# Six staggered weight tiles, a padded activation pitch, split first loads and dummy products in a two-layer encoder on one core

## The chip, the core and the metric

The kernel runs on one core of a Trainium2 chip. That core has five engines that run side by side and tell each other by semaphores when a tile is ready: TensorE (PE in the profile; its weight loads stand on a row of their own, PEld), VectorE (DVE), ScalarE (ACT), GpSimd (POOL) and SyncE (SP), which here only issues the transfers from the chip's memory. TensorE multiplies a stationary operand, which a weight load has put into its array, with a moving operand, and adds into an accumulation bank (PSUM). All other tiles lie in the on-chip memory SBUF, 128 partitions wide; an address in this text is a byte offset within a partition.

The metric is device time in microseconds (us), the median over three runs: 1684.95 us before (1684.54 to 1685.41).

## The reference

The input is 256 positions of 2048 channels, in float32. Two layers follow each other; the part of the reference that sets the work is the sequence of projections:

```python
h = rms_norm(x, norm_w[0])
a_q, a_i, a_ff, a_fb, a_g, b_u, b_g = split_cols(h @ w_in, EV_SIZES)   # 7 x 2048 columns
a_out = hgrn2_mixer(a_q, a_i, a_ff, a_fb, lb, hgrn_nw) * silu(a_g)     # chunked gated recurrence
b_out = fourier_mixer(b_u, fw, fb) * silu(b_g)                         # Re(DFT2), then a map per group
x = x + concatenate([a_out, b_out]) @ w_out                            # 4096 -> 2048
h = rms_norm(x, norm_w[1])
c_in, c_b, c_c, c_g, d_z, d_xbc, d_dt = split_cols(h @ w_in, OD_SIZES)
c_out = c_b * conv3(c_c * c_in) * silu(c_g)
d_out = ssd_mixer(d_xbc, d_dt, d_z, ...)                               # Mamba-2 scan, both directions
x = x + concatenate([c_out, d_out]) @ w_out
return rms_norm(x, final_norm_w)
```

Every weight is used once for all 256 positions, so 314 MB of weights pass through the core, and the four large projections are nearly all of the arithmetic.

## The kernel before

**Products in two parts.** TensorE multiplies in a single-pass form of float32 with fewer bits (`float32r`). To keep the accuracy, a weight tile is split into `hi`, its rounded value, and `lo`, the rest; an activation is split in the same way into `s = 0` and `s = 1`. A product is hi times both parts and lo times the first. The activations of a layer lie in `xx` (16 channel tiles, each with 2 parts of 256 positions, 2048 bytes per tile), the inputs of an output projection in `mm` (32 such tiles).

**The weight ring.** The weights come in halves of 128 x 1024 numbers (512 KB), 562 in all, in the order of the list `halves`. `load()` issues the transfer of one half into one of 5 raw tiles. `fetch()` makes hi on ScalarE (L132) and lo on VectorE (L133), into one of 3 pairs, the ring: hi0, lo0, hi1, lo1, hi2, lo2. `half()` hands out the next pair and runs `fetch()` up to 4 halves ahead. A pair is written again only when TensorE has read it, and a raw tile when lo is made. The last eight halves use three further pairs from the pool `fin`.

**The three streams of products.** `gemm_half` (L164, L167) uses the weights as stationary operand: 8 products with hi and 512 moving columns (both parts of `xx`), then 8 with lo and 256 columns. 402 halves go this way. `tproduct` (L183), the output projections, has `mm` stationary and the weights moving, 12 products of 512 columns per half, 128 halves. The value projection (L508) has `xx` stationary, 12 products per half, 32 halves; its first eight halves are the kernel's first work.

**What sets the order.** The code is written as one sequence; each engine takes its own instructions from it in an order that the build lays down, and waits in that order. `later(n, fn)` puts small work (scores, transposes, convolutions, norms) n halves behind the place where it is written. Transfers are all issued by SyncE, in order, on a set of eight completion semaphores, so that a transfer also waits until the one eight issues ahead of it has landed.

**The start.** L258 to L271: the parameters, then four raw halves and eight x tiles of two channel tiles each. For every x tile, `split_by` makes the scaled activation `xx` on ScalarE (L223) and its remainder on VectorE (L224). In between `norm0` squares the x tiles on ScalarE (L276), and small tables of the lower bounds (L310 to L319) are made on VectorE, with an exponential on ScalarE (L314).

**Addresses.** In the built program every raw, hi and lo tile (4096 bytes each), `xx`, `mm`, `conT`, the t1 tiles (1024 bytes) and the larger working tiles start at a multiple of 512 bytes. The tile `fill` (L69) is not used by any instruction; it moves the pools behind it to such a multiple. `acT` holds, among others, the sine table `sl`, whose two parts start 8 and 4 bytes past a multiple of 512.

Of the kernel before, what the change touches and what calls it, by code (L numbers as in the profile page):

```python
# [8 lines left out]
F32 = mybir.dt.float32  # L9
F32R = mybir.dt.float32r  # L10
U32 = mybir.dt.uint32
AF = mybir.ActivationFunctionType
ALU = mybir.AluOpType
ADD, SUB, MUL, MIN, MAX = ALU.add, ALU.subtract, ALU.mult, ALU.min, ALU.max

P = 128
D = 2048
L = 256
KT = D // P
# [37 lines left out]
def encoder_kernel(ctx: ExitStack, tc, xT, xN, w_ev, w_evo, w_od, w_odo, fw, fnr, par, con, acon, tric, outN):  # L57
    nc = tc.nc
    V, S, PE = nc.vector, nc.scalar, nc.tensor

    cpool = ctx.enter_context(tc.tile_pool(name="cpool", bufs=1))
    wpool = ctx.enter_context(tc.tile_pool(name="wpool", bufs=1))
    tp = ctx.enter_context(tc.tile_pool(name="tp", bufs=1))
# [6 lines left out]

    parT = cpool.tile([P, NPAR], F32, tag="par", name="parT")
    conT = cpool.tile([P, NCON], F32, tag="con", name="conT")
    xx = cpool.tile([P, KT, 2, L], F32R, tag="xx", name="xx")
    mm = cpool.tile([P, 2 * KT, 2, L], F32R, tag="mm", name="mm")
    epsT = sp.tile([P, 1], F32, tag="eps", name="epsT")
    x1d = dpool.tile([2, P, D], F32, tag="x1d", name="x1d")
# [2 lines left out]
    def pcol(name, i):  # L79
        return parT[:, PCOL[name] + i:PCOL[name] + i + 1]  # L80
# [4 lines left out]
    lpool, N2, NPM = [], 8, 4  # L85

    def t1(name, n=L):
        return tp.tile([P, n], F32, tag="t1", name=name, bufs=18)

    def t2(name, shape=(2, L)):  # L90
        return lpool[0].tile([P, *shape], F32, tag="t2", name=name, bufs=N2)

    def psum(tag, name, bufs, shape=(512,)):
        return ps.tile([P, *shape], F32, tag=tag, name=name, bufs=bufs)
# [4 lines left out]
    def paux(name, shape=(512,)):  # L99
        return psum("px", name, 8 - NPM, shape)  # L100
# [4 lines left out]
    n = 2 * (112 + 32)  # L105
# [2 lines left out]
    state = {"load": 0, "next": 0, "use": 0}  # L108
    HK = KT // 2
    NRAW, NHL, AHEAD = 5, 3, 4  # L110
    endp = []

    def load():
        n = state["load"]
        state["load"] = n + 1
        src, i, h = halves[n]
        raw = wpool.tile([P, HK * P], F32, tag=f"raw{n % NRAW}", name=f"raw{n}")
        nc.sync.dma_start(out=raw, in_=src[i][:, h * HK * P:(h + 1) * HK * P])
        loaded[n] = raw

    def fetch():
        n = state["next"]
        state["next"] = n + 1
        if n >= state["load"]:
            load()
        raw = loaded.pop(n)
        kept = n - (len(halves) - 8)
        i = n % NHL if kept < 0 else kept % (2 * NHL)
        pool = wpool if i < NHL else endp[0]
        hi = pool.tile([P, HK * P], F32R, tag=f"hi{i}", name=f"hi{n}")  # L130
        lo = pool.tile([P, HK * P], F32R, tag=f"lo{i}", name=f"lo{n}")
        S.activation(hi, raw, AF.Copy)  # L132
        V.tensor_tensor(lo, raw, hi.bitcast(F32), SUB)  # L133
        ready[n] = (hi, lo)

    def later(n, fn):
# [15 lines left out]
    def half():  # L152

        n = state["use"]
        due(n)
        while state["next"] <= min(n + AHEAD, len(halves) - 1):
            fetch()
        state["use"] = n + 1
        return ready.pop(n)
# [46 lines left out]
    def total(name, p):  # L206

        u = t1(f"{name}_u")
        S.activation(u, p[:, L:], AF.Copy)
        V.tensor_tensor(u, p[:, :L], u, ADD)  # L210
        return u
# [5 lines left out]
    def split_by(dst, src, w=None):  # L217

        if w is None:
            S.activation(dst[:, 0], src, AF.Copy)  # L220
            V.tensor_tensor(dst[:, 1], src, dst[:, 0].bitcast(F32), SUB)
        else:
            S.activation(dst[:, 0], src, AF.Copy, scale=w)  # L223
            V.scalar_tensor_tensor(dst[:, 1], src, w, dst[:, 0].bitcast(F32), MUL, SUB)  # L224
# [20 lines left out]
    def silu(name, z):  # L245
        e = t1(f"{name}_e")
        S.activation(e, z, AF.Exp, scale=-1.0)
        V.tensor_scalar(e, e, BIG, None, MIN)
        S.activation(e, e, AF.Ln, bias=1.0)
        S.activation(e, e, AF.Exp, scale=-1.0)  # L250
        V.tensor_tensor(e, e, z, MUL)
        return e
# [2 lines left out]
    lay = ExitStack()  # L255
    ap_ = lay.enter_context(tc.tile_pool(name="ap", bufs=1))
    lpool.append(ap_)
    nc.sync.dma_start(out=parT, in_=par)  # L258
    V.memset(epsT, EPS)
    xcs = []  # L260
    for c in range(8):
        if c % 2 == 0:
            load()
        xc = t2(f"x{c}")
        nc.sync.dma_start(out=xc, in_=xT[:, 2 * c:2 * c + 2, :])
        xcs.append(xc)
    for c in range(8):
        if c % 2 == 0:
            fetch()
        for k in range(2):  # L270
            split_by(xx[:, 2 * c + k], xcs[c][:, k, :], pcol("nw0", 2 * c + k))  # L271
    rs = {}

    def norm0():
        for c in range(8):
            S.activation(xcs[c], xcs[c], AF.Square)  # L276
        for n in (4, 2, 1):
            for c in range(n):
                V.tensor_tensor(xcs[c], xcs[c], xcs[c + n], ADD)
        rs["sq"] = t1("sq_x")  # L280
        V.tensor_tensor(rs["sq"], xcs[0][:, 0, :], xcs[0][:, 1, :], ADD)
# [14 lines left out]
    with lay:  # L296
# [203 lines left out]
        for hp in range(8):  # L500
            if hp % 2 == 0:
                pv = [pmain(f"pv{hp}_{b}") for b in range(2)]
                for u in range(8):
                    hi, lo = half()
                    for k in range(2):
                        for b in range(2):
                            for n, (s_, w) in enumerate(((0, hi), (0, lo), (1, hi))):
                                PE.matmul(pv[b], lhsT=xx[:, 2 * u + k, s_, b * P:(b + 1) * P],  # L508
                                          rhs=w[:, k * 4 * P:(k + 1) * 4 * P], start=(u == 0 and k == 0 and n == 0),
                                          stop=(u == 7 and k == 1 and n == 2))  # L510
# [5 lines left out]
            for i in range(2):  # L516
                h = 2 * hp + i
# [15 lines left out]
            for i in range(2):  # L533
                h = 2 * hp + i
# [6 lines left out]


    ss1 = sp.tile([P, 2, 4], F32, tag="ss1", name="ss1")
    ones = cpool.tile([P, P], F32, tag="ones", name="ones")
    nc.gpsimd.memset(ones, 1.0)
    op = ctx.enter_context(tc.tile_pool(name="op", bufs=1))

    def tok(name, bufs=4):
        return op.tile([P, 4 * P], F32, tag="tok", name=name, bufs=bufs)
# [10 lines left out]
    for g in range(4):  # L560
# [7 lines left out]
        for b in range(2):  # L568
            V.tensor_tensor(x1[b], x1[b], po[b], ADD)
            nc.sync.dma_start(out=x1d[b, :, g * 4 * P:(g + 1) * 4 * P], in_=x1[b])  # L570
            s = tok(f"x1s{g}_{b}", 4)
# [213 lines left out]


    fin = ctx.enter_context(tc.tile_pool(name="fin", bufs=1))
    xf = cpool.tile([P, KT, 2, L], F32, tag="xx", name="xf").rearrange("p a b c -> p (a b c)")
    x2, fnT = xf[:, :2 * D].rearrange("p (b n) -> p b n", b=2), xf[:, 2 * D:3 * D]
    nc.sync.dma_start(out=fnT, in_=fnr.partition_broadcast(P))  # L790
    endp.append(fin)
# [142 lines left out]
```

## Time and profile before

| | |
|---|---|
| median of three runs | 1684.95 us (1684.54 to 1685.41) |
| the profiled execution's own time | 1684.59 us |
| its span, first to last instruction | 1682.8 us |
| TensorE busy, products | 1666.2 us, 9216 recorded |
| VectorE busy | 1247.6 us |
| ScalarE busy | 950.2 us |
| read from memory | 313.77 MB, 189 GB/s over the span with what is written |

A span is what the profiler saw of the program; the execution's own time includes some 1.8 us around it. Products are recorded longer than they hold TensorE, since the next one starts while the last one drains; the pace is therefore read from the starts. A float32 product that is not of the form `float32r` appears as two records.

### The profile page before, as it was taken

Reading aid. Unit: us, or ns where it says so; the run is one execution under the profiler, and the core shown is the slowest. Engines: PE = TensorE matmul, PEld = TensorE weight load, DVE = VectorE, ACT = ScalarE, POOL = GpSimd, SP = SyncE. Lnnn points to the kernel's source line nnn. Section 1 sums busy time; section 2 is a strip of 40 time slices with the busy share of each in tenths; the row PEclk is TensorE's granted clock in tenths of the full one; section 3 lists DMA queues with packets and bytes.
Section 4 is the critical chain, followed back from the end, with each engine's and each line's share of the span. In section 5 each row is a group of like instructions: output and inputs, shape, how many; then the busy total and the mean of one; then the engine's idle time right before and its main releaser. Section 6 shows DMA issues by size and latency. Waiting matters only on the chain.

```text
span 1682.8 us, 24794 instructions
## 1 busy us (share of the span) xinstructions
PE 1666.2 (99%) x9216; PEld 1443.0 (86%) x9216; DVE 1247.6 (74%) x2187; ACT 950.2 (56%) x1593; POOL 1.8 (0%) x13
## 2 busy tenths in 40 slices
PE   8999999999999999999999999999999999999997
PEld 6888888888888888888888888888888888888886
DVE  7868677867786788754548998888898797865554
ACT  6656555655665565644445576666665565654443
POOL 0000000000000000000000000000000000000000
PEclk9999999999999999999999999999999999999999
DMA  8555555545445545476665667656656655576553
GB/s 304 173 179 174 167 171 179 171 167 186 166 158 180 191 154 178 158 223 206 213 212 191 205 218 200 195 191 203 197 185 201 196 193 179 178 238 209 195 192 123
DMA packets 97977, 319.65 MB, mean 190 GB/s; under 512 B 10880, under 2 KB 19520, under 8 KB 97728
## 3 DMA queue, kind: packets, MB, share of 16 engines
q1 hardware_dynamic: 97856, 318.07, 57.5%
q8 instruction: 72, 1.18, 0.3%
q14 instruction: 49, 0.40, 0.1%
HBM read 313.77 MB, written 4.26 MB: 189 GB/s over the span
## 4 chain that ended last, share of the span: by engine, by line
PE 99%; DMA 0%; ACT 0%; DVE 0%; ACTq 0%; issue 0%; SPq 0%
PE pz L164 10%; PE o L183 10%; PE pz L167 5%; PE pv L508 5%; PE oD L183 5%; PE oC L183 5%; PE px L164 4%; PE pbg L164 4%; PE pq L164 4%; PE pcb L164 4%; PE pu L164 4%; PE pci L164 4%; PE pcg L164 3%; PE pcc L164 3%; PE pg L164 3%; PE pci L167 2%
## 5 line engine op out<-in xcount | busy, mean ns | idle before, releaser
L133 DVE TENSOR_TENSOR lo<-raw,hi 128x1024 fp32r<-128x1024 f32 x562 | 686.0, 1223 | 383.1 <-ACT hi L132 379.4
L132 ACT ACTIVATE hi<-raw 128x1024 fp32r<-128x1024 f32 x562 | 594.8, 1059 | 552.7 <-PE o L183 88.4
L164 PE MATMUL pz<-xx,hi 128*128 128x512 f32 x768 | 192.4, 393 | 0.0
L164 PEld LDWEIGHTS pz<-xx,hi 128*128 128x128 f32 x768 | 138.2, 189 | 24.5
L183 PE MATMUL o<-hi,mm 128*128 128x512 f32 x512 | 126.9, 390 | 0.0
L183 PEld LDWEIGHTS o<-hi,mm 128*128 128x128 f32 x512 | 95.8, 188 | 19.7
L167 PEld LDWEIGHTS pz<-xx,lo 128*128 128x128 f32 x768 | 104.8, 191 | 7.5
L167 PE MATMUL pz<-xx,lo 128*128 128x256 f32 x768 | 107.1, 283 | 0.0
L508 PE MATMUL pv<-hi,xx 128*128 128x512 f32 x256 | 81.9, 399 | 7.0 <-ACT xx L223 7.0
L183 PE MATMUL o<-lo,mm 128*128 128x512 f32 x256 | 68.5, 389 | 0.0
L164 PE MATMUL pbg<-xx,hi 128*128 128x512 f32 x256 | 66.2, 400 | 0.0
L164 PE MATMUL pcb<-xx,hi 128*128 128x512 f32 x256 | 65.5, 398 | 0.0
L164 PE MATMUL pg<-xx,hi 128*128 128x512 f32 x256 | 65.4, 398 | 0.0
L164 PE MATMUL px<-xx,hi 128*128 128x512 f32 x256 | 65.3, 397 | 0.0
L164 PE MATMUL pu<-xx,hi 128*128 128x512 f32 x256 | 64.8, 395 | 0.0
L164 PE MATMUL pci<-xx,hi 128*128 128x512 f32 x256 | 64.8, 395 | 0.0
L183 PE MATMUL oC<-hi,mm 128*128 128x512 f32 x256 | 64.5, 389 | 0.0
L164 PE MATMUL pq<-xx,hi 128*128 128x512 f32 x256 | 64.5, 394 | 0.0
L164 PE MATMUL pcc<-xx,hi 128*128 128x512 f32 x256 | 64.1, 393 | 0.0
L164 PE MATMUL pcg<-xx,hi 128*128 128x512 f32 x256 | 64.1, 393 | 0.0
L508 PEld LDWEIGHTS pv<-hi,xx 128*128 128x128 f32 x256 | 49.2, 192 | 17.3 <-ACT xx L223 7.0
L183 PE MATMUL oD<-hi,mm 128*128 128x512 f32 x256 | 63.4, 390 | 0.0
(551 smaller groups left out, 2851.0 us busy)
## 6 DMA issues: line engine op xcount, KB each, us to landing
raw<-in_w_ev SPq DMA_DIRECT2D x224, 512.0 KB, 3.9
raw<-in_w_od SPq DMA_DIRECT2D x210, 512.0 KB, 4.4
raw<-in_w_evo SPq DMA_DIRECT2D x64, 512.0 KB, 4.5
raw<-in_w_odo SPq DMA_DIRECT2D x64, 512.0 KB, 4.5
ab<-rd SPq DMA_DIRECT2D x64, 128.0 KB, 4.9
x<-in_xT SPq DMA_DIRECT2D x8, 256.0 KB, 6.9
fw<-in_fw SPq DMA_DIRECT2D x8, 256.0 KB, 5.9
xr<-in_xN SPq DMA_DIRECT2D x8, 256.0 KB, 5.8
```

What stands on the lines that cost most here:

```text
L132: S.activation(hi, raw, AF.Copy)
L133: V.tensor_tensor(lo, raw, hi.bitcast(F32), SUB)
L164: PE.matmul(out, lhsT=hi[:, k * P:(k + 1) * P], rhs=a[:, k0 + k].rearrange("p s n -> p (s n)"), start=(first and k == 0), stop=False)
L167: PE.matmul(out[:, :L], lhsT=lo[:, k * P:(k + 1) * P], rhs=a[:, k0 + k, 0], start=False, stop=(last and k == HK - 1))
L183: PE.matmul(outs[b], lhsT=a[:, k0 + 2 * u + k, s_, b * P:(b + 1) * P], rhs=w2[part][:, k * 4 * P:(k + 1) * 4 * P], start=(u == 0 and part ...
L508: PE.matmul(pv[b], lhsT=xx[:, 2 * u + k, s_, b * P:(b + 1) * P], rhs=w[:, k * 4 * P:(k + 1) * 4 * P], start=(u == 0 and k == 0 and n == 0) ...
```

## The change

Four things are changed together.

1. The six ring tiles get paddings (`HLPAD`), so that in the built program they start at 0, 32, 64, 128, 256 and 96 bytes past a multiple of 512 (hi0, lo0, hi1, lo1, hi2, lo2). The raw tiles, `mm` and the last three pairs stay at multiples of 512.
2. `xx` gets 8 unused numbers per channel tile: a pitch of 2080 bytes instead of 2048, so that tile k starts at 32 k bytes past a multiple of 512, and the sixteen tiles have sixteen offsets. To make room, the t1 pool shrinks from 18 tiles to 16.
3. The first raw half is loaded, rounded and subtracted in two pieces of 512 columns; the first x tile is loaded in two pieces, and of the parameters first only the 16 columns of the first norm.
4. `ones` is set by VectorE at the start (before: by GpSimd, later in the code), and TensorE runs 16 float32 products of `ones` with itself into an accumulation tile that nobody reads.

```diff
+    XS = 2 * L + 8
+    xx = cpool.tile([P, KT, XS], F32R, tag="xx", name="xx")[:, :, :2 * L].rearrange("p k (s n) -> p k s n", s=2)
...
-        return tp.tile([P, n], F32, tag="t1", name=name, bufs=18)
+        return tp.tile([P, n], F32, tag="t1", name=name, bufs=16)
...
+    HLPAD = ((8, 8), (16, 32), (88, 104))
+
+    def pieces(n):
+        return (slice(0, 512), slice(512, 1024)) if n == 0 else (slice(0, 1024),)
...
-        nc.sync.dma_start(out=raw, in_=src[i][:, h * HK * P:(h + 1) * HK * P])
+        for c in pieces(n):
+            nc.sync.dma_start(out=raw[:, c], in_=src[i][:, h * HK * P + c.start:h * HK * P + c.stop])
...
-        hi = pool.tile([P, HK * P], F32R, tag=f"hi{i}", name=f"hi{n}")
-        lo = pool.tile([P, HK * P], F32R, tag=f"lo{i}", name=f"lo{n}")
-        S.activation(hi, raw, AF.Copy)
-        V.tensor_tensor(lo, raw, hi.bitcast(F32), SUB)
+        ph, pl = HLPAD[i] if i < NHL else (0, 0)
+        hi = pool.tile([P, HK * P + ph], F32R, tag=f"hi{i}", name=f"hi{n}")[:, :HK * P]
+        lo = pool.tile([P, HK * P + pl], F32R, tag=f"lo{i}", name=f"lo{n}")[:, :HK * P]
+        for c in pieces(n):
+            S.activation(hi[:, c], raw[:, c], AF.Copy)
+            V.tensor_tensor(lo[:, c], raw[:, c], hi[:, c].bitcast(F32), SUB)
...
-    nc.sync.dma_start(out=parT, in_=par)
+    ones = cpool.tile([P, P], F32, tag="ones", name="ones")
+    V.memset(ones, 1.0)
     V.memset(epsT, EPS)
+
+    warm = paux("warm")
+    for i in range(16):
+        PE.matmul(warm[:, :P], lhsT=ones, rhs=ones, start=True, stop=True)
+    nc.sync.dma_start(out=parT[:, :16], in_=par[:, :16])
     xcs = []
     for c in range(8):
         if c % 2 == 0:
             load()
         xc = t2(f"x{c}")
-        nc.sync.dma_start(out=xc, in_=xT[:, 2 * c:2 * c + 2, :])
+        for k in (slice(0, 1), slice(1, 2)) if c == 0 else (slice(0, 2),):
+            nc.sync.dma_start(out=xc[:, k], in_=xT[:, 2 * c + k.start:2 * c + k.stop, :])
         xcs.append(xc)
+        if c == 1:
+            nc.sync.dma_start(out=parT[:, 16:], in_=par[:, 16:])
...
-    xf = cpool.tile([P, KT, 2, L], F32, tag="xx", name="xf").rearrange("p a b c -> p (a b c)")
+    xf = cpool.tile([P, KT, XS], F32, tag="xx", name="xf").rearrange("p k n -> p (k n)")
```

In the built program the order of the instructions differs only at the start; from the sixth half on every engine's sequence is the same as before.

ScalarE's first instructions before, up to the third hi, with the semaphores that each waits for (DMAHW a landing, DVE VectorE; `aneg` and `lbe` are the exponentials of small parameters, `x` at L276 the squares):

```order
L644 ACTIVATE aneg<-parT 64x1 [waits DMAHW0_49]
L314 ACTIVATE lbe<-lbe 128x48 [waits DVE_49]
L132 ACTIVATE hi_110<-raw_86 128x1024 [waits DMAHW1_49]
L223 ACTIVATE xx<-x_88,parT 128x256 [waits DMAHW2_49]
L223 ACTIVATE xx<-x_88,parT 128x256
L223 ACTIVATE xx<-x_90,parT 128x256 [waits DMAHW3_49]
L223 ACTIVATE xx<-x_90,parT 128x256
L276 ACTIVATE x_88<-x_88 128x512 [waits DVE_49]
L132 ACTIVATE hi_122<-raw_92 128x1024 [waits DMAHW4_49]
```

And now, to the second hi (L141 is the rounding, L232 the scaled activation, L294 the squares, L332 and L660 the exponentials):

```order
L141 ACTIVATE hi_132<-raw_105 128x512 [waits DMAHW1_49]
L141 ACTIVATE hi_132<-raw_105 128x512 [waits DMAHW2_49]
L232 ACTIVATE xx<-x_108,parT 128x256 [waits DMAHW3_49,DMAHW0_49]
L232 ACTIVATE xx<-x_108,parT 128x256 [waits DMAHW4_49]
L232 ACTIVATE xx<-x_111,parT 128x256 [waits DMAHW5_49]
L232 ACTIVATE xx<-x_111,parT 128x256
L294 ACTIVATE x_108<-x_108 128x512 [waits DVE_49]
L660 ACTIVATE aneg<-parT 64x1 [waits DMAHW6_49]
L294 ACTIVATE x_111<-x_111 128x512 [waits DVE_49]
L332 ACTIVATE lbe<-lbe 128x48 [waits DVE_49]
L141 ACTIVATE hi_146<-raw_114 128x1024 [waits DMAHW7_49]
```

The first hi is in two pieces, and the two exponentials and a second square have moved from their earlier places to between the first activations and the second hi; the exponential `lbe` there waits for VectorE.

SyncE's first transfers before, up to the second raw half (raw are weights, x the input):

```order
L258 DMA parT<-in_par 128x352
L118 DMA raw_86<-in_w_ev 128x1024
L265 DMA x_88<-in_xT 128x512
L265 DMA x_90<-in_xT 128x512
L118 DMA raw_92<-in_w_ev 128x1024
```

And now:

```order
L274 DMA parT<-in_par 128x16
L125 DMA raw_105<-in_w_ev 128x512 x2
L281 DMA x_108<-in_xT 128x256 x2
L281 DMA x_111<-in_xT 128x512
L284 DMA parT<-in_par 128x336
L125 DMA raw_114<-in_w_ev 128x1024
```

The second raw half is now the eighth transfer and was the fifth; the bytes ahead of it are the same.

## Rows read from the trace of the kernel before

**Rows 1.** the page's engines: busy us (share of the span), instructions

```profile
PE 1666.2 (99%) x9216; PEld 1443.0 (86%) x9216; DVE 1247.6 (74%) x2187; ACT 950.2 (56%) x1593; POOL 1.8 (0%) x13
```

**Rows 2.** the page's chain that ended last, by engine

```profile
PE 99%; DMA 0%; ACT 0%; DVE 0%; ACTq 0%; issue 0%; SPq 0%
```

**Rows 3.** the page's costliest groups: xcount | busy us, mean ns | idle before

```profile
L164 PE MATMUL pz<-xx,hi 128*128 128x512 f32 x768 | 192.4, 393 | 0.0
...
L183 PE MATMUL o<-hi,mm 128*128 128x512 f32 x512 | 126.9, 390 | 0.0
```

**Rows 4.** timeline, TensorE, 949.86 to 952.70: start us, length us, instructions

```profile
949.85 2.00 PE L164 MATMUL pci<-xx,hi 128*128 128x512 f32 x8
951.69 1.12 PE L167 MATMUL pci<-xx,lo 128*128 128x256 f32 x8
952.65 0.40 PE L164 MATMUL pcc<-xx,hi 128*128 128x512 f32 x1
```

**Rows 5.** stretches: length, then busy us of PE, PEld, DVE, ACT, POOL

```profile
949.85:951.69 1.84, 1.84 (x10) 1.51 (x9) 0.00 (x0) 1.16 (x3) 0.00 (x0) 1.00 0.51 95
581.54:583.38 1.84, 1.84 (x10) 1.51 (x9) 1.84 (x8) 1.67 (x4) 0.00 (x0) 1.00 0.63 207
951.69:952.64 0.95, 0.95 (x9) 0.94 (x8) 0.45 (x2) 0.00 (x0) 0.00 (x0) 1.00 0.60 165
451.86:452.81 0.95, 0.95 (x9) 0.94 (x8) 0.29 (x1) 0.95 (x6) 0.00 (x0) 1.00 0.76 254
1560.38:1562.19 1.81, 1.81 (x9) 1.50 (x8) 0.09 (x2) 1.06 (x1) 0.00 (x0) 1.00 0.48 174
```

**Rows 6.** groups by line and shape, TensorE, as in Rows 3

```profile
L381 PE MATMUL sb<-q,k 128*128 128x128 f32 x64 | 12.4, 275 | 0.0
...
L470 PE MATMUL fm<-acT,fP 128*128 128x127 f32 x32 | 4.9, 274 | 0.0
```

**Rows 7.** timeline, TensorE, 161.3 to 162.1, float32 products

```profile
161.51 0.39 PE L375 MATMUL sa<-DQ,D 128*128 128x128 f32 x2
...
161.96 0.39 PE L375 MATMUL sa<-DQ,D 128*128 128x128 f32 x2
```

**Rows 8.** timeline, ScalarE, 0 to 30

```profile
5.50 1.06 ACT L132 ACTIVATE hi<-raw 128x1024 fp32r<-128x1024 f32 x1 [1.37 <-DMA raw<-in_w_ev]
...
9.17 1.04 ACT L132 ACTIVATE hi<-raw 128x1024 fp32r<-128x1024 f32 x1
...
18.37 1.05 ACT L132 ACTIVATE hi<-raw 128x1024 fp32r<-128x1024 f32 x1
...
26.21 1.06 ACT L132 ACTIVATE hi<-raw 128x1024 fp32r<-128x1024 f32 x1 [1.66 <-PE pv L508]
```

**Rows 9.** timeline, TensorE, 6.9 to 8.5 and 20.3 to 21.3

```profile
7.00 1.22 PE L508 MATMUL pv<-hi,xx 128*128 128x512 f32 x2 [7.00 <-ACT xx L223]
8.03 0.64 PE L508 MATMUL pv<-lo,xx 128*128 128x512 f32 x1
8.46 0.63 PE L508 MATMUL pv<-hi,xx 128*128 128x512 f32 x1
...
20.34 0.84 PE L508 MATMUL pv<-hi,xx 128*128 128x512 f32 x3
21.02 0.39 PE L508 MATMUL pv<-lo,xx 128*128 128x512 f32 x1
```

**Rows 10.** stretches of the start: as Rows 5, then granted clock, DMA, GB/s

```profile
0.00:7.00 7.00, 0.00 (x0) 0.00 (x0) 2.18 (x14) 3.23 (x6) 1.52 (x12) 1.00 0.71 215
7.00:12.20 5.20, 5.20 (x12) 3.96 (x13) 4.35 (x9) 4.71 (x10) 0.00 (x0) 1.00 0.99 349
```

**Rows 11.** timeline, VectorE, 0 to 30

```profile
19.45 1.23 DVE L133 TENSOR_TENSOR lo<-raw,hi 128x1024 fp32r<-128x1024 f32 x1 [0.26 <-ACT hi L132]
```

**Rows 12.** timeline, SyncE, 0 to 60: issues of transfers

```profile
1.18 0.41 SPq L118 DMA_DIRECT2D raw<-in_w_ev  x1
...
2.59 0.43 SPq L118 DMA_DIRECT2D raw<-in_w_ev  x1
```

More of the change, by code (lines that the diff above doesn't have):

```diff
@@ L72, in encoder_kernel @@
     conT = cpool.tile([P, NCON], F32, tag="con", name="conT")
-    xx = cpool.tile([P, KT, 2, L], F32R, tag="xx", name="xx")
+    XS = 2 * L + 8
+    xx = cpool.tile([P, KT, XS], F32R, tag="xx", name="xx")[:, :, :2 * L].rearrange("p k (s n) -> p k s n", s=2)
     mm = cpool.tile([P, 2 * KT, 2, L], F32R, tag="mm", name="mm")
@@ L543, in encoder_kernel @@
     ss1 = sp.tile([P, 2, 4], F32, tag="ss1", name="ss1")
-    ones = cpool.tile([P, P], F32, tag="ones", name="ones")
-    nc.gpsimd.memset(ones, 1.0)
     op = ctx.enter_context(tc.tile_pool(name="op", bufs=1))
```

## Prediction

> **What bounds the kernel now.** I read the page's table of engines first, then the chain of waits. TensorE is busy for 99% of the span [rows 1], and the chain that ended last is 99% TensorE [rows 2]: after its first product it never stands still for another engine, so a gain must come from the pace of its products or from the start. The profiled execution took 1684.6 us for a span of 1682.8, and the three timed runs have a median of 1684.95, 0.4 above it; I work out differences from the trace and set them against the median. Less than 0.2%, 3.4 us, I call no change, since no measurement of this kernel tells it apart.
>
> The work is three streams of 128x512 or 128x256 products. By the code, 402 halves go through `gemm_half`, each with 8 products of 512 columns (L164) and 8 of 256 (L167), 3216 of each; 128 halves go through `tproduct` (1536 products, L183) and 32 through the value projection (384, L508). That is 8352 in all; two of the costliest groups show their recorded lengths, 393 and 390 ns [rows 3]. These lengths overlap, so the pace is read from start to start. In the timeline 8 products of L164 take from 949.85 to 951.69, 1.84 us, and the 8 of L167 behind them 0.95 [rows 4].
>
> **The offsets and the pitch: 0.** All ring tiles, activations, raw tiles and working tiles now start at multiples of 512 bytes. The change can help in two ways. The first: ScalarE writes a hi tile and VectorE a lo tile while TensorE reads others, and they hinder each other at equal offsets. The table by stretches tests that directly [rows 5]. Eight L164 products take 1.84 us with VectorE at 0.00 and also with VectorE busy in all of it and ScalarE in 1.67. Eight L167 products take 0.95 us with ScalarE at 0.00 and with ScalarE busy throughout. Eight of L183 take 1.81 us beside 1.06 us of ScalarE. I see no sign of engines hindering TensorE at today's equal offsets, so I cost this at nothing.
>
> The second way: TensorE's weight load and its own moving read meet at equal offsets. No row shows two alignments of these products, so it is bounded from both sides. At 2.4 GHz and a column a cycle, 512 columns are 213 ns; 1.81 us / 8 is 226, so 13 ns are over, and for 256 columns 0.95 / 8 - 107 = 12. If all of it and the 1.84 - 1.81 = 0.03 us per half came from alignment, 5136 x 13 + 3216 x 12 + 402 x 30 ns = 117 us would go. For a loss, the nearest row is the sine table: its moving rows start 4 or 8 bytes past a multiple of 512, and its 127-column products last 274 ns against 275 for 128 aligned columns [rows 6], so an offset costs within 1 ns there, 8 us over 8352 products. The widest spread of equal shapes is 30 ns in eight, 4 ns each, or 33 us: my other end. Between -117 and +33 I take 0. The nearest row is an aligned one: four fp32 records (161.51 to 161.96) [rows 7] take 112 ns for 256 columns, only 5 over, although weights and moving tile also start at multiples of 512. And the 13 ns are the same for 512 and 256 columns, as a fixed cost per product would be; a collision should follow how long both read.
>
> The Trainium skill speaks to this in "SBUF — State Buffer", section "Who interferes with whom": TensorE has two independent read ports, one for the moving operand and one for the weight load, and it never waits for another engine. [rows 5] agree for the other engines (1.84 us either way); for TensorE against itself no run here shows it. By that rule this part is exactly 0.
>
> **The start: -0.3 us.** Before, the first raw tile lets ScalarE start at 5.50 [rows 8] and the first product stands at 7.00 [rows 9]. The first half's products are 0.43 us apart (8.03 and 8.46) and later 0.227 (three from 20.34 to 21.02) [rows 9]: half pace, TensorE's 1.2 GHz level as I read it from the spacing, until about 12.2, which is 5.2 us after it began. The granted clock column prints 1.00 there [rows 10], so the spacing decides.
>
> The change makes the first halves of loads land sooner and lets TensorE run 16 dummy products. In the program each is one row, in the trace an fp32 product is two records 0.11 us apart [rows 7]: 32 records, 3.6 us at full pace, 7.2 at half. They start near 1.0 and end between 4.6 and 8.2, so the first real product comes between 6.0 and 8.2, at full pace.
>
> What of it survives? The pacemaker of the start is not TensorE. From the second hi (9.17) ScalarE works without a gap to the fifth (18.37 + 1.05): three rounds of 3.07 us [rows 8]. VectorE ends the fifth lo at 19.45 + 1.23 = 20.68 [rows 11], and TensorE's fifth half wants it at 21.02, its third product [rows 9]. That slack of 0.34 us is all TensorE can gain unless the second hi comes earlier: what it wins before, it waits for at 20.68. Not until 26.21 does ScalarE wait for TensorE (1.66 us) [rows 8], so everything up to there is paced by that round. The changed order keeps these rounds row by row.
>
> When does the second hi start? Ahead of it stand the same bytes (parameters 0.18 MB, first raw 0.52, two x tiles 0.52, its own 0.52: 1.75 MB); at 215 GB/s to 7.0 us and 349 behind it [rows 10] they are there at 7.7 at the earliest. SyncE issues three transfers more ahead of it, some 0.47 us each (three intervals from 1.18 to 2.59, which was its issue) [rows 12]: about 4.0, still long before. On ScalarE two squares, the parameter exponentials and the halves, 4.4 us of work, now stand ahead of it: from a first landing near 4, 8.4. And the second of these exponentials now waits for VectorE's small chain behind the four xx remainders: up to about 9.8. So 8.4 to 9.8, and I take today's 9.17. With the slack the start gives -0.3 us, between -1.1 and +0.3.
>
> The rest: `ones` is set by VectorE before it has work. The t1 pool goes from 18 to 16; behind the start the rows of ScalarE and VectorE stand as before and no waiting kind is added, and a late scratch tile is hidden by VectorE's free quarter [rows 1]. If that cover is gone, a gate's chain runs late and TensorE waits for a PSUM bank. I cost both at 0.
>
> Sum: 1684.95 - 0.3 = 1684.6.
>
> **Rivals.**
> - *Products after narrow ones lose their extra time* (22%). L164 has 1.84 us per eight where L183 has 1.81; if the pitch is what costs the 0.03, 402 x 0.03 = 12 us go: 1673. For: the excess stands in the one line where the xx tiles move and the ring is stationary. Against: the same line keeps it whatever the other engines do.
> - *Weight load and moving read do collide* (13%). Of the 117 us I take half, since sixteen offsets of xx cannot all miss a tile: 58 us, 1626. For: 13 ns in every one of 8352 products. Against: [rows 7].
> - *The warm start counts in full* (3%). First product 1.0 us sooner and 12 x (0.43 - 0.227) = 2.4: 3.4 us, 1681.5. The Trainium skill's page "TensorE: Matmul & The Clock Gate", section "What's actually happening", says that activity releases the throttle; the doubling of the pace after 7.00 agrees (0.43 to 0.227 us). Against: the round of 3.07 us sets the fifth half anyway.
> - *Slower: operands off the 512 grid* (20%). A weight slice of 512 bytes then covers parts of two aligned stretches, and a moving read five instead of four. At 1 ns for each of 8352 products it is 8 us, 1693; at 4 ns 1718. It decides from 0.4 ns per product. For: five of six ring tiles and fifteen of sixteen xx slices move off. Against: the sine table's row.
>
> My forecast, addresses without effect and a start held by the load rounds, has 42%; its own range is 1683.5 to 1686. Faster by over 0.2% is the first three rivals, 38%; slower 20%; within it 42%. The range goes from 1655, which leaves out the second rival and little else, to 1695, which leaves out the dearer part of the last.
>
> **What would show it.** Right: eight L164 products again in 1.84 us, eight L167 in 0.95, eight L183 in 1.81; products of the first half 0.227 apart; a gap on TensorE before its second half, and the fifth lo still ending near 20.7. Wrong: L183 below 1.81 or L167 below 0.95 (collision), L164 alone at 1.81 (first rival), all higher by 8 ns or more in eight (slower), or the fifth lo a microsecond off.

## The result: 16 us slower

| | before | after |
|---|---|---|
| median of four runs, us | 1684.97 (1684.54 to 1685.41) | 1700.95 (1700.49 to 1701.27) |
| ratio, 95% interval | | 1.0095 [1.0077, 1.0112] |
| profiled execution, span, us | 1684.6, 1682.8 | 1700.49, 1698.7 |

The prediction said 1684.6, no change, between 1655 and 1695; the kernel is slower by 16 us and lies above that range. The page of the changed kernel, engines and then the chain by engine, answers to [rows 1, 2]; the two groups of products below answer to [rows 3]:

```profile
PE 1685.6 (99%) x9248; PEld 1444.4 (85%) x9248; DVE 1248.5 (73%) x2189; ACT 950.5 (56%) x1594; POOL 1.7 (0%) x12
...
PE 98%; ACT 0%; DMA 0%; DVE 0%; SPq 0%; issue 0%; ACTq 0%; DVEq 0%
...
L173 PE MATMUL pz<-xx,hi 128*128 128x512 f32 x768 | 194.5, 395 | 0.0
...
L192 PE MATMUL o<-hi,mm 128*128 128x512 f32 x512 | 128.7, 393 | 0.0
```

TensorE is still the bound (99% busy) and stands still hardly more than before, so its products must come further apart. Their recorded lengths hide most of that: 395 and 393 ns where [rows 3] have 393 and 390. The timeline of TensorE in the same channel as [rows 4] (start us, length, instructions) and stretches as in [rows 5] show the spacing:

```profile
959.91 2.04 PE L173 MATMUL pci<-xx,hi 128*128 128x512 f32 x8
961.78 1.10 PE L176 MATMUL pci<-xx,lo 128*128 128x256 f32 x8
962.73 0.63 PE L173 MATMUL pcc<-xx,hi 128*128 128x512 f32 x2
```

```profile
959.91:961.78 1.87, 1.87 (x10) 1.51 (x9) 0.00 (x0) 1.13 (x3) 0.00 (x0) 1.00 0.39 72
961.78:962.73 0.95, 0.95 (x10) 0.94 (x9) 0.84 (x3) 0.00 (x0) 0.00 (x0) 1.00 0.82 198
790.49:798.82 8.33, 8.33 (x37) 6.77 (x36) 3.68 (x3) 3.18 (x4) 0.00 (x0) 1.00 0.55 187
```

Eight L173 products take 1.87 us instead of 1.84, with VectorE idle and the clock at 1.00. The third stretch is three whole halves of `tproduct`, 36 products; the same three before:

```profile
782.70:790.86 8.16, 8.16 (x37) 6.75 (x36) 3.68 (x3) 3.18 (x4) 0.00 (x0) 1.00 0.60 193
```

VectorE and ScalarE did the same 3.68 and 3.18 us of work beside both, and TensorE needed 0.17 us more. Averaged over all products of a stream behind the start of the program, from each product's start to the start of the next one, in ns: `gemm_half`'s 512 columns 232.7 before and 235.6 after, its 256 columns 119.5 and 118.3, `tproduct` 227.2 and 231.8, the value projection 228.1 and 232.9. Times 3216, 3216, 1536 and about 300 products that is +9.3 - 3.9 + 7.1 + 1.4 = +13.9 us.

The rest is lost in the start. ScalarE's hi rows, TensorE, and stretches, which answer to [rows 8, 9, 10]:

```profile
4.65 1.27 ACT L141 ACTIVATE hi<-raw 128x512 fp32r<-128x512 f32 x2 [2.63 <-DMA raw<-in_w_ev]
...
10.55 1.06 ACT L141 ACTIVATE hi<-raw 128x1024 fp32r<-128x1024 f32 x1 [0.27 <-DMA raw<-in_w_ev]
12.39 1.71 ACT L232 ACTIVATE xx<-x,parT 128x256 fp32r<-128x256 f32 x4 [0.79 <-DMA x<-in_xT]
...
20.66 1.04 ACT L141 ACTIVATE hi<-raw 128x1024 fp32r<-128x1024 f32 x1
```

```profile
1.05 6.39 PE L273 MATMUL warm<-ones 128*128 128x128 f32 x32 [1.05 <-DVE epsT L269]
7.20 0.48 PE L526 MATMUL pv<-hi,xx 128*128 128x512 f32 x1
...
7.74 0.63 PE L526 MATMUL pv<-hi,xx 128*128 128x512 f32 x2
8.20 0.40 PE L526 MATMUL pv<-lo,xx 128*128 128x512 f32 x1
...
11.66 0.73 PE L526 MATMUL pv<-hi,xx 128*128 128x512 f32 x2 [1.44 <-ACT hi L141]
...
13.25 0.61 PE L526 MATMUL pv<-hi,xx 128*128 128x512 f32 x1
13.66 0.63 PE L526 MATMUL pv<-lo,xx 128*128 128x512 f32 x1
...
23.27 0.50 PE L526 MATMUL pv<-lo,xx 128*128 128x512 f32 x1 [0.19 <-DVE lo L142]
```

```profile
0.00:7.00 7.00, 5.95 (x30) 5.95 (x31) 1.86 (x6) 3.48 (x6) 1.37 (x11) 1.00 0.64 179
7.00:12.20 5.20, 3.76 (x18) 2.65 (x17) 3.47 (x17) 3.32 (x7) 0.00 (x0) 1.00 0.93 310
12.20:17.80 5.60, 5.07 (x15) 3.88 (x15) 4.55 (x9) 5.41 (x12) 0.00 (x0) 0.70 1.04 412
```

The dummies do their work: the first half runs at full pace from 7.20 (two products in 0.46 us from 7.74). But 179 GB/s were moved up to 7.0 us instead of 215. The second raw half is issued at 4.01 us instead of 2.59 and lands 6.5 us behind its issue (before 6.4), so near 10.5 instead of 9.0, and ScalarE's second hi, which waits for it, starts at 10.55 instead of 9.17. TensorE waits, and behind the wait its clock is granted at 0.70 over 12.2 to 17.8, with products 0.41 us apart at first (13.25, 13.66), the 1.2 GHz level. The fifth hi starts at 20.66 instead of 18.37, and the fifth half's first lo product at 23.27 instead of 21.02. Later halves stay about 2.4 us late (the sixth begins at 25.72; before, 23.29). 13.9 + 2.4 = 16.3 us, against 16.0 measured.

### The profile page after: what moved, and what is told of

Same layout as the page of the kernel before. It is cut to its first block, busy times and chain, and to the rows that moved or that the text cites. A ratio compares the mean times of both kernels' runs of the same rounds, so it can differ in the third digit from the quotient of the medians.

```text
span 1698.7 us, 24867 instructions
## 1 busy us (share of the span) xinstructions
PE 1685.6 (99%) x9248; PEld 1444.4 (85%) x9248; DVE 1248.5 (73%) x2189; ACT 950.5 (56%) x1594; POOL 1.7 (0%) x12
## 4 chain that ended last, share of the span: by engine, by line
PE 98%; ACT 0%; DMA 0%; DVE 0%; SPq 0%; issue 0%; ACTq 0%; DVEq 0%
PE pz L173 11%; PE o L192 10%; PE pz L176 5%; PE oD L192 5%; PE oC L192 5%; PE pv L526 5%; PE px L173 4%; PE pq L173 4%; PE pcb L173 4%; PE pcg L173 4%; PE pbg L173 4%; PE pu L173 4%; PE pci L173 4%; PE pcc L173 4%; PE pg L173 4%; PE pg L176 2%
## 5 line engine op out<-in xcount | busy, mean ns | idle before, releaser
L142 DVE TENSOR_TENSOR lo<-raw,hi 128x1024 fp32r<-128x1024 f32 (+1 forms) x563 | 687.1, 1223 | 398.1 <-ACT hi L141 391.0
L141 ACT ACTIVATE hi<-raw 128x1024 fp32r<-128x1024 f32 (+1 forms) x563 | 595.1, 1057 | 569.3 <-PE o L192 91.5
L173 PE MATMUL pz<-xx,hi 128*128 128x512 f32 x768 | 194.5, 395 | 0.0
L173 PEld LDWEIGHTS pz<-xx,hi 128*128 128x128 f32 x768 | 137.7, 188 | 25.6
L173 PE MATMUL pbg<-xx,hi 128*128 128x512 f32 x256 | 66.8, 403 | 0.0
L173 PE MATMUL pcb<-xx,hi 128*128 128x512 f32 x256 | 66.2, 401 | 0.0
L173 PE MATMUL pg<-xx,hi 128*128 128x512 f32 x256 | 66.0, 400 | 0.0
L173 PE MATMUL px<-xx,hi 128*128 128x512 f32 x256 | 65.9, 399 | 0.0
L173 PE MATMUL pu<-xx,hi 128*128 128x512 f32 x256 | 65.5, 398 | 0.0
L173 PE MATMUL pci<-xx,hi 128*128 128x512 f32 x256 | 65.5, 398 | 0.0
L173 PE MATMUL pq<-xx,hi 128*128 128x512 f32 x256 | 65.2, 397 | 0.0
L173 PE MATMUL pcg<-xx,hi 128*128 128x512 f32 x256 | 64.9, 395 | 0.0
L173 PE MATMUL pcc<-xx,hi 128*128 128x512 f32 x256 | 64.8, 395 | 0.0
```

The source lines that it names most:

```text
L141: S.activation(hi[:, c], raw[:, c], AF.Copy)
L142: V.tensor_tensor(lo[:, c], raw[:, c], hi[:, c].bitcast(F32), SUB)
L173: PE.matmul(out, lhsT=hi[:, k * P:(k + 1) * P], rhs=a[:, k0 + k].rearrange("p s n -> p (s n)"), start=(first and k == 0), stop=False)
```

## The experiments

Each run takes out some of the changes, or tries one variant of them, and is given as a ratio to the kernel before on the same chip. The t1 pool has 16 tiles where nothing else is said. The columns hi, lo and tproduct are mean ns from start to start: 512 and 256 columns in `gemm_half`, and `tproduct`.

| run | time us | ratio, interval | hi | lo | tproduct |
|---|---|---|---|---|---|
| e1 start alone | 1687.42 | 1.0017 [1.0008, 1.0026] | 232.7 | 119.5 | 227.2 |
| e2 six ring offsets | 1695.56 | 1.0069 [1.0054, 1.0084] | 234.2 | 118.8 | 231.8 |
| e3 pitch | 1696.77 | 1.0074 [1.0057, 1.0090] | 236.3 | 119.1 | 227.2 |
| e4 ring at 32 | 1704.55 | 1.0120 [1.0105, 1.0135] | 235.5 | 119.3 | 233.6 |
| e5 ring, xx, mm at 32 | 1685.02 | 1.0002 [0.9992, 1.0011] | 232.8 | 119.5 | 227.5 |
| e6 ring at 256 | 1684.68 | 1.0000 [0.9990, 1.0009] | 232.7 | 119.5 | 227.3 |
| e7 scan | 1691.82 | 1.0042 [1.0027, 1.0057] | 234.2 | 117.5 | 232.3 |
| e15 xx, mm at 32 | 1700.74 | 1.0093 [1.0078, 1.0108] | 235.9 | 117.7 | 233.7 |
| e10 lo at 64 | 1678.90 | 0.9967 [0.9955, 0.9979] | 232.7 | 117.7 | 227.2 |
| e11 lo scan | 1681.24 | 0.9979 [0.9970, 0.9988] | 232.9 | 118.3 | 227.2 |
| e13 lo at 192 | 1683.93 | 0.9993 [0.9984, 1.0003] | 233.4 | 118.4 | 227.2 |
| e14 hi 128, lo 64 | 1680.02 | 0.9970 [0.9959, 0.9982] | 235.0 | 115.9 | 227.3 |
| e8 start, parameters first | 1686.63 | 1.0011 [1.0001, 1.0020] | 232.8 | 119.5 | 227.2 |
| e9 dummies alone | 1684.71 | 0.9999 [0.9990, 1.0007] | 232.8 | 119.5 | 227.2 |
| e12 split loads alone | 1686.50 | 1.0010 [1.0001, 1.0019] | 232.7 | 119.5 | 227.4 |

### One part at a time: e1, e2, e3

e1 is the changed kernel without offsets and pitch:

```diff
-    XS = 2 * L + 8
+    XS = 2 * L
-    HLPAD = ((8, 8), (16, 32), (88, 104))
+    HLPAD = ((0, 0), (0, 0), (0, 0))
```

> The changed start alone (split first loads, split parameters, 16 dummy products, t1 pool of 16), all tiles at multiples of 512 as before. In the changed kernel the first lo product of the fifth half stands at 23.27 us instead of 21.02, so if the start is a cost of its own this kernel is 2 to 2.5 us slower than before (1687.2) and its products keep the old pace (L173 eight in 1.84 us, L192 twelve in 2.72). Rival: the start costs nothing by itself and the late fifth half came from the slower products of the first halves: within 0.5 us of before. Rival of the prediction, a warm start that counts in full: 1681.5.

e2 has only the ring's paddings (`HLPAD` as in the change), e3 only the pitch (`XS = 2 * L + 8`).

> The six ring offsets alone, pitch 2048 and the old start. Settling theory (a run of products reaches 226.7 ns only after some ten products whose offsets don't change, and each change of tile starts that over): the output projections, which change tile every eight and four products, get their whole loss, 7 us, the value projection about 2, and the 402 halves with a constant offset inside hi lose only at the changes, 0 to 5 us: 1692 to 1699. Off-the-grid theory (an operand that doesn't start at a multiple of 512 costs a fixed time): L164 loses 5 of 6 of what it lost in the changed kernel, 9 us, and hi0 halves lose nothing while hi1 and hi2 do. Theory of the other engines (staggering moves collisions with what ScalarE and VectorE write): all of the address loss, 13.6 us: 1698.6.

> The pitch of 2080 bytes alone, ring at multiples of 512, old start. Settling theory: the moving offset changes with every product of L164 and L167, so eight hi products take about 1.86 instead of 1.84 us and eight lo products 0.94 instead of 0.95: 402 x (20 - 11 ns) = 4 us slower, and the output projections keep 2.72 us per half exactly: 1689. Off-the-grid theory: fifteen of sixteen moving tiles are off, lo loses as well as hi. Theory of the other engines: xx is written only at the start and between the layers, so this kernel is 0 to 0.5 us off before.

All three are slower: about 3, 11 and 12 us. The products of e1 keep the pace of the kernel before (first row of the table), so its 3 us are the start alone. The sum, 27, is more than the change's 16, so ring and pitch don't simply add. Where each bites is plain in one stretch: a `tproduct` half in e2, then a `gemm_half` of eight and a `tproduct` half in e3 (columns as before).

```profile
801.06:803.83 2.77, 2.77 (x14) 2.20 (x12) 1.23 (x1) 1.67 (x4) 0.00 (x0) 1.00 0.83 224
```

```profile
976.09:977.96 1.87, 1.87 (x11) 1.51 (x9) 1.87 (x5) 1.61 (x2) 0.00 (x0) 1.00 0.64 239
800.45:803.17 2.72, 2.72 (x14) 2.25 (x12) 2.21 (x3) 1.74 (x4) 0.00 (x0) 1.00 0.82 273
```

`tproduct` multiplies ring tiles with `mm`. The ring's offsets slow it (2.77 us for twelve; before 2.72, a third of the 8.16 above); the pitch of `xx`, which it does not touch, leaves it alone. In e3 every ring tile that ScalarE and VectorE write lies where it lay before, and `gemm_half` is slower all the same, so what these engines write into the ring is not the cause there. For `tproduct` e15 and e5 below show the same.

### Absolute or relative: e4, e5, e15, e6

e4 moves all ring tiles by the same 32 bytes; e5 moves `xx` and `mm` by 32 as well; e15 moves `xx` and `mm` alone (t1 pool 17); e6 moves the ring by 256. Further unused tiles, not shown, bring what lies behind back to a multiple of 512.

```diff
+        if n == 0:
+            wpool.tile([P, 8], F32, tag="sh0", name="sh0")    # e4, e5; e6: 64 instead of 8
+    cpool.tile([P, 8], F32, tag="sh2", name="sh2")            # e5, e15: ahead of xx
```

> All six ring tiles at 32 bytes past a multiple of 512, so the offsets against xx and mm are equal in every product but not zero; pitch 2048, old start. Settling theory: nothing changes from product to product, so the pace settles; if it settles at the same 226.7 ns the time is that of before within 1 us, and if the difference of offsets sets the settled pace, every group moves by one constant. Off-the-grid theory: every product pays the same price as in the changed kernel or more, 10 to 17 us slower. Theory of the other engines: hi, lo and raw differ now, no tile collides anew: as before within 1 us.

e4 refuted my first theory, that only changes of offset between tiles cost and a constant one does not: 20 us.

> Before with the six ring tiles and also xx and mm moved to 32 bytes past a multiple of 512; only the raw tiles and the scratch stay. Theory A, what counts is how the weight tile lies relative to the moving tile: both are moved alike, tproduct settles at 227 ns again and the time is 1684 to 1686. Theory B, what counts is that an operand itself lies off the grid: with both operands off it, at least the 20 us of the ring alone at 32 bytes, 1704 or more. Rival C, only the ring's own offset counts, whichever operand it is: 1704 again, not more.

> The reverse of the ring at 32 bytes: xx and mm at 32 bytes past a multiple of 512, all ring tiles on the grid. If the offset of the one operand relative to the other is what counts: slower by about as much as the ring at 32 alone, 1700 to 1707, tproduct near 233 ns. If only the ring's own offset counts (and the kernel with all at 32 was as fast as before for another reason): 1684 to 1686, tproduct 227.

> Before with all six ring tiles at 256 bytes past a multiple of 512, everything else as it was. If the pace depends on the offset modulo 256 (in the kernels with six offsets, halves whose hi lies at 256 settled at 227 ns like those at 0): tproduct 227 ns, 1684 to 1687. If any offset off the grid of 512 costs what 32 bytes cost: 1700 to 1705.

Stretches of e4, e5 and e15: eight hi products, eight lo products, and one `tproduct` half.

```profile
980.07:981.93 1.86, 1.86 (x10) 1.51 (x9) 1.86 (x5) 1.61 (x2) 0.00 (x0) 1.00 0.55 186
981.93:982.88 0.95, 0.95 (x9) 0.95 (x8) 0.95 (x2) 0.84 (x2) 0.00 (x0) 1.00 0.26 79
802.13:804.93 2.80, 2.80 (x13) 2.25 (x12) 2.19 (x3) 1.74 (x4) 0.00 (x0) 1.00 0.84 261
```

```profile
980.08:981.92 1.84, 1.84 (x11) 1.50 (x9) 1.84 (x5) 1.79 (x4) 0.00 (x0) 1.00 0.87 249
981.92:982.87 0.95, 0.95 (x9) 0.95 (x8) 0.95 (x3) 0.84 (x2) 0.00 (x0) 1.00 0.59 237
802.30:805.02 2.72, 2.72 (x13) 2.25 (x12) 1.23 (x1) 1.11 (x2) 0.00 (x0) 1.00 0.56 203
```

```profile
977.57:979.44 1.87, 1.87 (x10) 1.50 (x9) 1.87 (x5) 1.61 (x2) 0.00 (x0) 1.00 0.50 138
979.44:980.38 0.94, 0.94 (x10) 0.94 (x8) 0.94 (x2) 0.87 (x2) 0.00 (x0) 1.00 0.32 105
802.85:805.65 2.80, 2.80 (x13) 2.21 (x12) 1.23 (x1) 1.67 (x4) 0.00 (x0) 1.00 0.91 252
```

For a shift of 32 bytes this settles it. With one operand 32 bytes off, whichever, a `tproduct` half takes 2.80 us; with both off by the same, 2.72, as on the grid. What counts is the offset of the weight tile relative to the activation tile that it is multiplied with. A relative offset of 256 bytes (e6) is as good as 0. The t1 pool of 16, which e5 and e6 have too, costs nothing.

### Which relative offsets: e7, e10, e11, e13, e14

e7 slices hi at 128, 192 and 16 bytes and lo at 64, 256 and 16, by ring tile (t1 pool 15):

```diff
+        oh, ol = ((32, 16), (48, 64), (4, 4))[i] if i < NHL else (0, 0)
+        hi = pool.tile([P, HK * P + ...], ...)[:, oh:oh + HK * P]
+        lo = pool.tile([P, HK * P + ...], ...)[:, ol:ol + HK * P]
```

> Before with ring tiles at other offsets past a multiple of 512: hi at 128, 192 and 16 bytes, lo at 64, 256 and 16. It is a scan: the spacing of products by tile is what it is for. If the grid is 256, hi at 128, 192 and 16 bytes all settle above 229 ns in tproduct; if it is 128, the halves at 128 settle at 227 and the others do not; if it is 64, those at 128 and 192 settle at 227 and only 16 does not. The time is between 1690 and 1700 in the first case, 1688 to 1694 in the others, since changes between offsets cost by themselves.

No `tproduct` half at 128, 192 or 16 settled at 227 ns (medians of twelve 2796, 2782 and 2775 ns against 2720), so of the offsets tried only 256 is as good as 0, though in e7 each half also follows one at another offset. But the eight 256-column products of the tile with lo at 64 took 917 ns, less than the aligned 953. The next kernels shift only the halves that `gemm_half` uses as weights:

```diff
+    LOFF = (16, 16, 16)          # e11: (48, 12, 20); e13: (48, 48, 48)
+    def stationary(n):
+        return (n < 224 and n % 56 >= 8) or 288 <= n < 498
...
+        o = LOFF[i] if i < NHL and stationary(n) else 0
+        lo = pool.tile([P, HK * P + ...], ...)[:, o:o + HK * P]
+        hi = pool.tile([P, HK * P + ...], ...)[:, 2 * o:2 * o + HK * P]   # e14 only; t1 pool 15
```

> Before with the lo tiles of those halves alone that gemm_half uses as weights at 64 bytes past a multiple of 512; hi and all halves that tproduct and the values move stay at 0. In the scan, the halves with hi at 128 and lo at 64 took 917 ns for their eight 256-column products instead of 953. If the lo's own offset against xx does that: 402 x 36 ns = 14.5 us less, about 1670 (1668 to 1675, by what the change between hi and lo costs the first hi products). If it was the hi at 128 ahead of them: lo near 944 and hi near 1853 as in the kernel with six offsets, 1684 to 1687.

> As the kernel with lo at 64, but the three ring tiles at 192, 48 and 80 bytes. A scan: if only 64 (and by symmetry 192) is fast, those at 192 take about 917 ns for eight 256-column products and those at 48 and 80 take 930 to 950; if any offset that is no multiple of 256 is fast behind a hi at 0, all three take under 930. Time 1670 to 1686.

> As the kernel with lo at 64 (lo tiles of the halves that gemm_half uses), with the offset 192 for all three ring tiles. In the scan the half with lo at 192 took 1818 ns for its eight 512-column products (before: 1841) and 941 for the eight of 256 (before: 953), but it followed halves of other offsets. If the pace belongs to the pair of offsets: 402 x (23 + 12) = 14 us less, 1671. If what the earlier half left behind sets the first products: hi back at 1838 to 1850 and the time 1679 to 1682, as with 64.

> As the kernel with lo at 64, and in the same halves hi at 128 too; the halves that tproduct and the values move stay at 0. In the first scan this pair took 1857 ns for the eight 512-column products and 917 for the eight of 256, 2774 together against 2794 before and 2781 with lo at 64 alone. If the pace belongs to the pair of offsets: 402 x 20 ns = 8 us less than before, 1676 to 1678. If it came from the halves of other offsets around it: lo back near 943 and the time 1681 to 1686.

The stretches of e10, then of e14, eight hi and eight lo products each:

```profile
980.51:982.35 1.84, 1.84 (x11) 1.50 (x10) 1.84 (x5) 1.30 (x4) 0.00 (x0) 1.00 0.51 134
982.35:983.29 0.94, 0.94 (x10) 0.94 (x8) 0.94 (x3) 0.85 (x2) 0.00 (x0) 1.00 0.73 283
```

```profile
978.56:980.42 1.86, 1.86 (x11) 1.51 (x10) 1.86 (x5) 1.81 (x4) 0.00 (x0) 1.00 0.77 244
980.42:981.34 0.92, 0.92 (x10) 0.92 (x8) 0.92 (x3) 0.87 (x2) 0.00 (x0) 1.00 0.42 165
```

From start to start, medians over 308 undisturbed halves of each kernel, product by product:

```
before  233 236 229 232 231 227 227 226 | 113 119 120 120 120 120 120 120
e10     231 236 228 233 231 227 227 226 | 118 118 117 118 118 117 118 118
e14     226 230 232 241 232 231 232 233 | 122 116 114 113 113 113 113 118
e15     234 231 235 234 233 234 234 234 | 118 117 117 117 117 117 116 117
```

e10 is the best kernel of all, 6 us faster than before, but not the 14.5 that the first outcome promised: the same lo at 64 against the same `xx` runs at 118 ns behind a hi at 0 and at 113 behind a hi at 128. e14 repeated the scan's pair (1857 and 923 ns for eight; scan 1857 and 917; before 1841 and 953), and there the hi's loss takes back about half of what lo gains. In e11 the tile with lo at 192 took 1818 and 941; with all three at 192, in e13, it takes 1857 and 945, so what the earlier half left behind decides there. The 1818 belong to hi products at offset 0 behind a lo at 80: they stand 227 ns apart from the second on, so the slow first five of a half are not bound to be. The pace is thus no function of one product's two offsets alone; what came before it counts.

### The start: e8, e9, e12

e8 is e1 with the parameters loaded whole and first; e9 adds to the kernel before the 16 dummies alone; e12 is e8 without the dummies.

```diff
-    nc.sync.dma_start(out=parT[:, :16], in_=par[:, :16])
+    nc.sync.dma_start(out=parT, in_=par)                 # e8, e12
...
-    warm = paux("warm")                                  # e12
-    for i in range(16):
-        PE.matmul(warm[:, :P], lhsT=ones, rhs=ones, start=True, stop=True)
```

> The start of the changed kernel alone (dummies, first loads in halves; no offsets), but with the parameters loaded whole and first again, as before. If it is the rest of the parameters, late in the queue and waited for by ScalarE's second exponential and VectorE's small chain, that holds the second half of weights up: the second hi starts near 9.2 again, TensorE's fifth half no later than 21.1, and the time is 1683.5 to 1685. If the smaller first transfers themselves delay the second raw half: second hi again near 10.5 and 1687.4, as with the start alone.

> Before with the 16 dummy products alone: loads whole and in the old order, no offsets. The prediction's own reading of the start (the rounds of the loads set the fifth half, slack 0.34 us): first product at 7.0 and at 0.23 us pace, first half done near 9.8, the second hi at 9.2 as before, the fifth half's third product between 20.7 and 21.1, time 1684.0 to 1685. Rival, the dummies themselves cost (the clock falls in the wait behind the first half and the second half runs at 0.43 us, or the first product waits for them): the fifth half at 22 or later, 1686 to 1688.

> Before with the first raw half and the first x tile loaded and split in two pieces each, parameters whole and first, no dummies, no offsets. If the smaller first transfers are what makes the second raw half late: it lands near 10.3 us again (before: 8.99) and the time is 1686 to 1687. If it is the dummies: it lands at 9.0, second hi at 9.2, and the time is 1683.5 to 1685.

Stretches 0 to 7 and 12.2 to 17.8 of e9, then of e12, then of e8:

```profile
0.00:7.00 7.00, 5.95 (x28) 5.95 (x29) 2.23 (x15) 2.79 (x4) 1.37 (x11) 1.00 0.71 219
...
12.20:17.80 5.60, 5.35 (x23) 4.09 (x23) 4.88 (x10) 5.60 (x12) 0.00 (x0) 1.00 1.04 417
```

```profile
0.00:7.00 7.00, 0.00 (x0) 0.00 (x0) 2.46 (x15) 3.19 (x6) 1.37 (x11) 1.00 0.65 177
...
12.20:17.80 5.60, 5.34 (x23) 4.37 (x24) 4.97 (x11) 5.60 (x12) 0.00 (x0) 1.00 1.04 418
```

```profile
0.00:7.00 7.00, 5.19 (x32) 5.00 (x32) 2.68 (x15) 3.40 (x7) 1.38 (x11) 1.00 0.59 178
...
12.20:17.80 5.60, 4.73 (x20) 3.44 (x20) 5.04 (x10) 5.43 (x12) 0.00 (x0) 1.00 1.04 411
```

The kernels with whole first loads moved 215 and 219 GB/s by 7.0 us, those with split ones 177 to 179 (e1 168), with dummies or without. Their second hi starts late too: 9.17 before, 9.57 in e9, 10.11, 10.54 and 10.36 in e12, e8 and e1. So the split start is the cost, the loads in pieces together with the order on ScalarE that came with them: some 1.6 us by e12, whose interval only just leaves out 1. Which of the two it is stays open. In e12 the second raw half landed near 9.5 us (issue at 3.54, 6.0 to landing), as it did in e9 (2.59 and 7.0), in spite of 177 GB/s against 219; but ScalarE squared two x tiles ahead of the second hi where e9 squares one. ScalarE in e9, then in e12:

```profile
8.91 0.61 ACT L282 ACTIVATE x<-x 128x512 f32<-128x512 f32 x1
9.57 1.06 ACT L132 ACTIVATE hi<-raw 128x1024 fp32r<-128x1024 f32 x1
```

```profile
8.93 1.27 ACT L289 ACTIVATE x<-x 128x512 f32<-128x512 f32 x2
10.11 1.04 ACT L141 ACTIVATE hi<-raw 128x1024 fp32r<-128x1024 f32 x1
```

Of the two outcomes that e8's expectation names, its second hi (10.54) fits the second, while its time lies between e1 and before. The dummies neither help nor harm (e9), as the rounds of the loads set the pace. What splitting the parameters adds (e1 3.1 us over before, e8 1.9) is within the intervals; only e1 and the changed kernel, which have it, show the lower clock between 12.2 and 17.8 (0.72, 0.70). The landing times differ by parts of a microsecond between executions, and each is seen in one profile.

## Why the prediction was wrong

- **What bounds the kernel** was right: TensorE is busy for 99% of the span before and after. That the smaller t1 pool costs nothing was right too (e5, e6).
- **"The offsets and the pitch: 0"** is the step that failed, by 13.9 us. The bounds, -117 to +33, held it; the choice in them did not. What failed is the price "within 1 ns" that I gave an offset. I chose by the sine table's rows [rows 6]: its moving rows are 4 or 8 bytes off, and the products take the same time. Those are float32 products, two records each, at another offset than any that was tried later; the float32r products lose 6.4 ns of 227 at 32 bytes (e4). Whether the format or the small offset spares the float32 products, no run tells. I also read [rows 7] as evidence against a collision, again of float32 products; the rows print 128 columns, and the 256 that I counted for a record stand in none of them. And I compared recorded lengths, 274 and 275 ns, which hide most of a loss: `tproduct` records grew by 3 ns (390 to 393) as starts moved 4.6 apart. In the sine table's case the spacing would have misled me as well, since its records stand 111 ns apart on average and those of [rows 6]'s aligned line 112.
- Other engines don't hinder TensorE: that part stands. The Trainium skill's "SBUF — State Buffer", section "Who interferes with whom", has separate read ports for TensorE's moving operand and its weights; by that rule this part would be exactly 0. For other engines the trace agrees (the same 3.68 and 3.18 us beside 8.16 and 8.33). For TensorE against itself the measurement decides: two operands at 0 and 32 cost 16 to 20 us, both at 32 nothing.
- **Why the settled spacing depends on it** stays open. That weight loads and moving reads meet in a fixed rhythm would fit, since only their offset to each other counts, but this is not shown: no run shows the reads themselves, and the 256-column products are not fastest where the 512-column ones are.
- **"The start: -0.3 us"** was mis-sized: +2.4 by the rows above, 3 by e1. I bounded the second hi by 8.4 and 9.8, and it started at 10.55. The failed step is the landing of the second raw half. I had its bytes there at 7.7 at the earliest, from the GB/s before, and took ScalarE's own work for the bound; it landed near 10.5, and ScalarE waited for it. The sum was short for the kernel before as well, where the half landed near 9.0. By 7.0 us 179 GB/s were moved and not 215, and the half was issued 1.4 us later; which of these made it late stays open, since e12, with 177, had it near 9.5. Behind it, ScalarE also waited 0.79 us for an x tile, which I had not counted. That the first half runs at full pace and TensorE then waits (1.44 us) was right, and so was it that the warm start by itself gains hardly anything (e9). The fifth lo ended near 23.2, where my sign of being right was 20.7.
- **The rivals.** The slower one had the sign, with 1 to 4 ns per product; measured are 13.9 us / 8352 = 1.7, though not in every stream: the 256-column products became 1.2 ns faster. Its mechanism, slices that cover more stretches of 512 bytes, is refuted by e5: ring, `xx` and `mm` off the grid by the same 32 are as fast as on it. "Products after narrow ones lose their extra time": the eight hi products begin 233 to 236 apart and settle at 227 on the grid, and off it they never settle (e15), so it went the other way. The collision rival looked at the right pair of operands, but for 512 columns the grid is the good case and not the bad one: no offset settled below its 227 ns. For 256 columns there are offsets that gain, 8 to 36 ns in eight. The warm start that counts in full is refuted by e9, 1684.71 against 1684.92.

## What to carry to other kernels

Choose the offset of a weight tile relative to the activation tile that it meets, not each on its own; for 512 columns the relative offsets that cost nothing here were 0 and 256 bytes. Before padding "for variety", measure one constant shift of one operand and of both. Read products from start to start: recorded lengths overlap and hide a few ns that, times 8352, are 16 us. Evidence on one number format and one offset need not hold for another. At the start, loads in pieces, with the order that they bring, can cost more than an early first piece gives.

## What the hardware showed unexpectedly

- float32r products of 512 columns settle at 226.7 ns (2720 for twelve) at a relative offset of 0 or 256 bytes and at 233 (2800) at 32, in either direction (e4, e15).
- 256-column products run at 120 ns aligned, 117 to 118 with the activations 32 bytes on (e15) or the weights 64 (e10), and 113 at 64 behind hi weights at 128 (e14). With the weights 32 on (e4) they average 119, so here the direction counts.
- Behind the narrower products the first five of 512 columns on the grid stand 229 to 236 ns apart, then they settle at 227 ("before" above). `tproduct` halves of e2 with hi at 256, which follow halves at other offsets, do the same: 226, 236, 228, 233, 231, then 227.
- A clock once granted in full was at 0.70 again behind a wait of TensorE that ended at 11.66 us, and not in e8, where a wait ended at 11.64 (1.00). By the profile the wait was 1.44 us in the changed kernel and 1.31 in e8 (in e1, 0.72 behind 1.82); what made the difference no run shows.
